# A decoder layer on one core: the causal convolution by three half-length filters, its tables and FF operands moved

## The chip, the core and the metric

The kernel runs on one core of one Trainium2 chip. Its time is device microseconds (us) of one launch, as the median of several runs; a profiled execution of the same program gives the trace. The engines are TensorE (PE; its weight loads are PEld), VectorE (DVE), ScalarE (ACT), GpSimd (POOL) and SyncE (SP), which here only issues DMAs. Each runs its own instructions in order and waits on semaphores that other engines raise.

## The reference

One layer over 1024 tokens with 1024 features, all in float32. Cut to what matters here:

```python
z = rms_norm(h, mix_norm_g) @ w_in                 # split into conv, mla, pool, gmlp columns
a, g = jnp.split(z_conv, 2, axis=-1)               # conv: 256 channels
y = a * jax.nn.sigmoid(g)
y = lax.conv_general_dilated(y, dw_w[:, None, :], window_strides=(1,), padding=[(30, 0)],
        feature_group_count=256, ...) + dw_b       # causal, 31 taps, each channel by itself
o_conv = jax.nn.silu(layer_norm(y, ln_g, ln_b)) @ pw_w
o_mla  = latent_attention(z_mla, cos(positions), sin(positions), ...)
o_pool, o_gmlp = multiscale_pool(z_pool, ...), spatial_gating(z_gmlp, ...)
h = h + concat(rms_norm of each group) @ w_out
h = h + square(relu(rms_norm(h) @ w_ff1)) @ w_ff2  # 1024 -> 4096 -> 1024
out = rms_norm(h, final_norm_g)
```

## The kernel before

Every matmul keeps float32 accuracy by three passes (`mm3`): each operand is split into a high part (a ScalarE copy) and a low part (a VectorE subtraction; `split`, lines 130 and 131, or `split_scaled`, 134 and 135), and high x high, high x low and low x high are summed in PSUM. So every weight slab and every activation that TensorE reads costs one ScalarE and one VectorE instruction first.

**Stage 1**, to about 395 us, is all that precedes the FF part. The input projections come group by group: convolution (tiles `zc`, gated by `conv_gate` into `ycv`), pooling (`zp`), gating (`zgm`, two 128-token tiles at a time by `z_mm`), latents (`zml`). Weights come through a ring of two raw buffers (`load_raw`) on SP's queue and are split into slots of a ring of ten (`wslot`). The convolution holds channels on partitions (two tiles of 128, index `i`) and tokens along the free axis, in two halves of 512 (`hf`). A tap is one fused multiply-add of up to 512 columns with a per-channel weight (`lag`, `conv_taps`, line 337). Of the 31 taps, lag 0 is a ScalarE instruction (`tap0`); of the second channel tile 7 taps of the first half and 13 of the second (`NPT`) are a ScalarE multiplication and a GpSimd addition each (`pool_taps`, lines 328 and 329); the other 100 are VectorE's. The taps of the first half need only the first half's gating. Then `conv_ln` (layer norm over channels: transposes to tokens, statistics, back), `conv_out` (the pointwise matrix `cw`), and `wo_tile(0, ...)`, the convolution group's share of the output projection. The pooling windows are sums by doubling on GpSimd (`addsh`, line 355). The rotary table `CS` is made of positions by ten elementwise instructions (lines 383 to 392), six of them on GpSimd, and is read by `latent_T` and `q_prep`.

In stage 1 the order on each engine is not written by hand: a planner takes the program's order as priority, `tc.high_priority(offset=n)` lifts a block by n, and it places whatever its own estimate of times says is ready. The calls stand in lines 1256 to 1466.

**The FF part** has an order written by hand (`run`, in steps of 12 matmuls 128x512 for the first product and 12 per output tile for the second). Each step issues, in this order: weight loads for eight steps ahead, the `post` of the step before (evictions), the operand splits of four steps ahead, its own `now` list, the `split` of the step before, its matmuls. The first product uses Strassen's seven products on 2x2 blocks: tokens in two halves, features in two halves. For the first 12 pairs of weight blocks, `early` runs the two products that need only the first tokens (steps 0 to 23). Meanwhile `hn_T1`, `hn_T1_split`, `combine` and `combine_split` make the other token operands. `f_relu` evicts and squares, `f_parts` splits the result into a tile `fst` and GpSimd's queue stores it (`fs`); `f_store` stores it unsplit (`fr`). `h_away` stores four tiles of h that are not needed for a while. The second product runs in chunks of four pairs (`Chunk`), whose operands are loaded on SP's queue: tokens `fs` (0, 1, 3), weights `w1` and `w2`, unsplit tokens `f1` and `f2`. The loads of the first chunk are spread over the last steps of the first product (`tail2`, `tail`).

## Time and profile before

| | us |
|---|---|
| median of 3 runs | 1042.67 (1041.95 to 1043.56) |
| the profiled execution | 1039.44 |
| its span, first to last instruction | 1037.7 |

The mean granted TensorE clock is 0.985 of full. Busy time of TensorE is modelled from pipelined matmuls, so that "busy" is not yet "at full rate"; a count of matmuls in a stretch says more. "Idle before" in a row of a group is the time that the engine stood idle just before these instructions, and the arrow names what ended it. In a row of waits, "A line <- B line" means that A stood until B was done.

### The profile page before, as it was taken

To read this page: it belongs to the slowest core of one execution; us is meant where nothing else is said; L and a number is where in the kernel's file an instruction comes from. 1 tells how busy PE (TensorE), PEld (TensorE's weight loads), DVE (VectorE), ACT (ScalarE), POOL (GpSimd) and SP (SyncE) were. 2 spreads that over 40 slices of the span, in tenths; PEclk is the share of its full clock that TensorE was granted. 3 is DMA by queue.
4 is the path that set the end of the run, shared out by engine and by line. 5 is a ranking of instruction groups with operands and counts; after the bars stand their busy time and mean duration, and the time that the engine had idled before them with its cause. 6 is when DMAs were issued, how large, how long until landed. Compare 5 with 4: busy or idle time off the path is not lost.

```text
span 1037.7 us, 13384 instructions
## 1 busy us (share of the span) xinstructions
PE 992.7 (96%) x4674; PEld 817.8 (79%) x4674; DVE 846.3 (82%) x1276; ACT 502.3 (48%) x937; POOL 246.8 (24%) x333
## 2 busy tenths in 40 slices
PE   9994899999999999988999999999999999999996
PEld 7883689888888887867888887887888888888885
DVE  5999999998888765987677775656998988988997
ACT  7641147556657765754545444453341431431424
POOL 0459558423232312222121111211000000000005
PEclk9997899999999999999999999999999999999998
DMA  9411015210002006866666675559858258258004
GB/s 334 165 56 37 32 54 185 82 41 23 19 1 82 1 1 216 298 246 219 235 217 230 233 235 185 220 181 414 337 189 298 82 181 306 81 180 326 1 1 163
DMA packets 49492, 165.71 MB, mean 160 GB/s; under 512 B 6032, under 2 KB 7952, under 8 KB 49424
## 3 DMA queue, kind: packets, MB, share of 16 engines
q1 hardware_dynamic: 36288, 119.68, 33.1%
q0 software_dynamic: 12992, 45.10, 11.1%
q8 instruction: 37, 0.61, 0.2%
q14 instruction: 31, 0.25, 0.1%
q10 hardware_dynamic: 144, 0.07, 0.0%
HBM read 113.45 MB, written 51.38 MB: 159 GB/s over the span
## 4 chain that ended last, share of the span: by engine, by line
PE 65%; DVE 16%; issue 6%; DMA 5%; ACT 4%; POOL 3%; SPq 0%; POOLq 0%; DVEq 0%; ACTq 0%
PE ffb L160 16%; PE ffx L160 13%; PE ffa L160 12%; DVE acc L337 8%; PE ffy L160 8%; PE wo L160 4%; PE ob L160 2%; PE s L676 2%; PE zc L160 2%; DMA raw_b<-in_w_ff 2%; DMA fs<-fst 1%; PE ptb L719 1%; PE woa L160 1%; PE qb L160 1%; DVE h L475 1%
## 5 line engine op out<-in xcount | busy, mean ns | idle before, releaser
L160 PE MATMUL ffb<-wop,fop 128*128 128x512 f32 x756 | 178.3, 395 | 0.0
L160 PEld LDWEIGHTS ffb<-wop,fop 128*128 128x128 f32 x756 | 142.1, 188 | 34.2
L160 PE MATMUL ffx<-hnT,wop 128*128 128x512 f32 x624 | 149.4, 392 | 0.8 <-DVE s L944 0.8
L160 PE MATMUL ffa<-wop,fop 128*128 128x512 f32 x576 | 137.3, 397 | 2.4 <-DVE h L1083 1.9
L160 PEld LDWEIGHTS ffx<-hnT,wop 128*128 128x128 f32 x624 | 117.0, 188 | 27.2 <-DVE s L944 1.2
L884 DVE TENSOR_TENSOR wop<-w_raw,wop 128x512 fp32r<-128x512 f32 x112 | 76.1, 688 | 68.3 <-ACT wop L881 68.3
L160 PEld LDWEIGHTS ffa<-wop,fop 128*128 128x128 f32 x576 | 109.2, 190 | 28.6 <-DVE h L1083 2.4
L881 ACT ACTIVATE wop<-raw_b 128x512 fp32r<-128x512 f32 x96 | 59.6, 623 | 122.9 <-PE ffa L160 44.3
L337 DVE SCALAR_TENSOR_TENSOR acc<-ycv,cols,acc 128x512 f32<-128x512 f32 (+22 forms) x100 | 99.1, 1032 | 0.7 <-ACT acc L317 0.4
L881 ACT ACTIVATE wop<-w_raw 128x512 fp32r<-128x512 f32 x112 | 68.8, 626 | 43.8 <-DVE w_raw L1027 18.9
L881 ACT ACTIVATE fop<-raw_f 128x512 fp32r<-128x512 f32 x64 | 39.8, 623 | 74.7 <-DVE h_back L1083 27.6
L160 PE MATMUL ffe<-hnT,wop 128*128 128x512 f32 x288 | 70.5, 402 | 4.4 <-ACT m L980 4.4
L1243 POOL TENSOR_SCALAR mr_ms<-mssq,epsr 128x1 f32<-128x1 f32 x7 | 2.8, 401 | 296.9 <-ACT fjunk L1241 296.9
L884 DVE TENSOR_TENSOR wop<-raw_b,wop 128x512 fp32r<-128x512 f32 x96 | 65.6, 684 | 9.3 <-ACT wop L881 8.6
L160 PEld LDWEIGHTS ffe<-hnT,wop 128*128 128x128 f32 x288 | 54.4, 191 | 17.0 <-ACT m L980 5.2
L160 PE MATMUL ffy<-hnB,wop 128*128 128x512 f32 x192 | 46.9, 393 | 2.8 <-ACT s L980 2.8
L160 PE MATMUL ffy<-hnT,wop 128*128 128x512 f32 x192 | 46.6, 391 | 0.0
L958 POOL DMA_DIRECT2D fs<-fst x48 | 25.8, 538 | 87.1 <-DVE fst L131 83.7
L160 PEld LDWEIGHTS ffy<-hnB,wop 128*128 128x128 f32 x192 | 36.0, 188 | 11.3 <-ACT s L980 3.2
L884 DVE TENSOR_TENSOR fop<-raw_f,fop 128x512 fp32r<-128x512 f32 x64 | 43.9, 686 | 0.0
L160 PEld LDWEIGHTS ffy<-hnT,wop 128*128 128x128 f32 x192 | 36.2, 189 | 8.1
L329 POOL TENSOR_TENSOR acc<-acc,tap 128x512 f32<-128x512 f32 (+7 forms) x20 | 35.0, 1749 | 28.9 <-ACT tap L328 27.6
(453 smaller groups left out, 2157.2 us busy)
## 6 DMA issues: line engine op xcount, KB each, us to landing
fs<-fst POOLq DMA_DIRECT2D x48, 512.0 KB, 3.4
fop<-fs SPq DMA_DIRECT2D x48, 512.0 KB, 7.2
w_raw<-in_w_ff SPq DMA_DIRECT2D x44, 512.0 KB, 4.4
raw_b<-in_w_ff SPq DMA_DIRECT2D x32, 512.0 KB, 5.9
raw_f<-fr SPq DMA_DIRECT2D x32, 512.0 KB, 5.7
fr<-s POOLq DMA_DIRECT2D x32, 256.0 KB, 3.2
fr<-f POOLq DMA_DIRECT2D x20, 256.0 KB, 2.4
xin<-in_x SPq DMA_DIRECT2D x8, 512.0 KB, 8.7
```

Of the source, the lines that this page charges most:

```text
L160: pe.matmul(out, lhs(x), rhs(y), start=start and i == 0, stop=stop and i == 2, skip_group_check=more)
L329: pool.tensor_tensor(aa, aa, tap, ALU.add)
L337: dve.scalar_tensor_tensor(aa, ya, c, aa, ALU.mult, ALU.add)
L475: dve.scalar_tensor_tensor(h[t], b, rs, h[t], ALU.mult, ALU.add)
L676: pe.matmul(sb_[:, c0:c0 + w], q[:, x, qo:qo + P], kt[:, y, 0:w], start=i == 0, stop=i == 2 and not last)
L719: pe.transpose(b[:, place[j] + s * P:place[j] + (s + 1) * P], pts[s][:, (2 * kp + j) * P:(2 * kp + j + 1) * P], ident)
L881: act.activation(self.t[:, 0], self.src(), AF.Copy)
L884: dve.tensor_sub(self.t[:, 1], self.src(), high(self.t))
L958: pool.dma_start(fs[p][q], t.rearrange("p x c -> p (x c)").bitcast(F32))
L1243: pool.tensor_scalar(ms, ssq, epsr[:, t:t + 1], 1.0, ALU.add, ALU.mult)
```

## The change

- **Convolution.** Even and odd tokens are kept as two planes of 512 (`conv_gate` writes them so, and builds the gate product in its PSUM bank). The even outputs are x0 * even taps + x1 (one step later) * odd taps; the odd outputs follow from (x0 + x1) * (even + odd taps) minus the two products. That makes three filters of 16, 15 and 16 taps over 512 columns per channel tile. All taps but two per tile run on VectorE; GpSimd has none. The block is placed, at normal priority, where the second half of the taps stood, and all four `conv_ln` after it; `cw` is loaded after them.
- **Position table.** Its six GpSimd instructions become six on VectorE.
- **Order of stage 1.** `gmlp(0)` stands after two more projections; two latent slabs (`zml` 2 and 3) use a raw buffer of another ring, and slab 3 has a higher priority.
- **FF.** `hn_T1` and its split run at steps 3 + 2j and 4 + 2j instead of 7 + 2j and 8 + 2j, `combine` and its split at 12 + 2j and 13 + 2j instead of 15 + 2j and 16 + 2j, `h_away` at step 4 instead of 5. The squaring of the early products goes from VectorE to ScalarE. `fst` of pairs 1 and 2 uses the ring of ten and not the single buffer `CS`. Of the first chunk's `fs` 1 loads, two go behind the `w2` loads.

```diff
-        dve.scalar_tensor_tensor(ycv[i][:, sl], ba, 0.5, rb[:, sl], ALU.mult, ALU.mult)
+        dve.scalar_tensor_tensor(ba, ba, 0.5, rb[:, sl], ALU.mult, ALU.mult)
         act.activation(th, th, AF.Tanh, scale=0.5)
-        dve.scalar_tensor_tensor(ycv[i][:, sl], th, 1.0, ycv[i][:, sl], ALU.add, ALU.mult)
+        dve.scalar_tensor_tensor(ycv[i].rearrange("p c n -> p n c")[:, hf * 256:(hf + 1) * 256],
+                                 th.rearrange("p (n c) -> p n c", c=2), 1.0,
+                                 ba.rearrange("p (n c) -> p n c", c=2), ALU.add, ALU.mult)
...
-    for hf in range(2):
-        tap0(0, hf)
-        tap0(1, hf)
-        pool_taps(hf, NPT[hf])
...
+    def conv_sums():
+        for i in range(2):
+            q = C_DWW + i * CK + 1
+            w = cols[:, q:q + CK - 1].rearrange("p (m c) -> p m c", c=2)
+            dve.tensor_add(hsum[:, i * (CK // 2):(i + 1) * (CK // 2)], w[:, :, 0], w[:, :, 1])
+
+    def chain(out, src, taps):
+        for k, c in taps:
+            dve.scalar_tensor_tensor(out[:, k:], src[:, 0:512 - k], c, out[:, k:], ALU.mult, ALU.add)
+
+    def conv_even_odd(i):
+        x0, x1 = ycv[i][:, 0], ycv[i][:, 1]
+        y0, y1 = acc[i][:, 0], acc[i][:, 1]
+        b = E("conv_b")
+        act.activation(y0, x0, AF.Copy, scale=tap(i, 0))
+        act.activation(b, x1, AF.Copy, scale=tap(i, 1))
+        chain(y0, x0, [(k, tap(i, 2 * k)) for k in range(1, CK // 2 + 1)])
+        chain(b, x1, [(k, tap(i, 2 * k + 1)) for k in range(1, CK // 2)])
+        bias = cols[:, C_DWB + i:C_DWB + i + 1]
+        dve.scalar_tensor_tensor(y1, y0, bias, b, ALU.subtract, ALU.add)
+        dve.tensor_scalar(y0[:, 0:1], y0[:, 0:1], bias, None, ALU.add)
+        dve.scalar_tensor_tensor(y0[:, 1:], y0[:, 1:], bias, b[:, 0:511], ALU.add, ALU.add)
+        dve.tensor_add(x0, x0, x1)
...
+        dve.scalar_tensor_tensor(y1, x0, both(0), y1, ALU.mult, ALU.subtract)
+        chain(y1, x0, [(k, both(k)) for k in range(1, CK // 2)] + [(CK // 2, tap(i, CK - 1))])
...
-    pool.tensor_scalar(ang, kq, cols[:, C_INVF:C_INVF + 1], 1.0, ALU.mult, ALU.mult)
-    pool.tensor_scalar(kq, ang, 1.0 / TWO_PI, cols[:, C_PHN:C_PHN + 1], ALU.mult, ALU.add)
-    pool.tensor_scalar(kq, kq, 1.0, MAGIC, ALU.mult, ALU.add)
-    pool.tensor_scalar(kq, kq, 1.0, -MAGIC, ALU.mult, ALU.add)
+    dve.tensor_scalar(ang, kq, cols[:, C_INVF:C_INVF + 1], None, ALU.mult)
+    dve.tensor_scalar(kq, ang, 1.0 / TWO_PI, cols[:, C_PHN:C_PHN + 1], ALU.mult, ALU.add)
+    dve.tensor_scalar(kq, kq, MAGIC, None, ALU.add)
+    dve.tensor_scalar(kq, kq, MAGIC, None, ALU.subtract)
...
-    pool.tensor_scalar(ang, ang, 1.0, cols[:, C_PHASE:C_PHASE + 1], ALU.mult, ALU.add)
-    pool.tensor_scalar(ang, ang, 3.1415925, -3.1415925, ALU.min, ALU.max)
+    dve.tensor_scalar(ang, ang, cols[:, C_PHASE:C_PHASE + 1], 3.1415925, ALU.add, ALU.min)
+    dve.tensor_scalar(ang, ang, -3.1415925, None, ALU.max)
...
+        if name == "zml" and s > 1:
+            raw = U("O", "zml_raw", [1024])
+            nc.sync.dma_start(raw[:, :2 * width], src[s])
+            wz[name, s] = split_w(raw, 2 * width, name + str(s))
...
         act.activation(f, b, AF.Relu)
-        if mul:
-            dve.tensor_mul(f, f, f)
-        else:
-            act.activation(f, f, AF.Square)
+        act.activation(f, f, AF.Square)
...
-                f_parts(p, 0, self.f, slot("fst") if p > 2 else
+                f_parts(p, 0, self.f, slot("fst") if p else
                         sb.tile([P, 2, 512], F32R, tag="CS", name="fst", bufs=1))
...
     with tc.high_priority(offset=2000):
-        conv_taps(0, NPT[0])
         z_load("zml", 2)
...
         load_wo(3, 0, dve)
+    with tc.high_priority(offset=4000):
         z_load("zml", 3)
     with tc.high_priority(offset=1000):
         load_wo(3, 1, pool)
-    with tc.high_priority(offset=300):
-        gmlp(0)
     z_mm("zgm", 1, 0)
     with tc.high_priority(offset=4000):
         z_mm("zml", 1, 1)
+    gmlp(0)
...
-    conv_ln(1)
-    with tc.high_priority(offset=4000):
-        conv_taps(1, NPT[1])
-        conv_ln(2)
+    conv_sums()
+    for i in range(2):
+        conv_even_odd(i)
+    for u in range(3):
+        conv_ln(u)
...
-        for f, s in ((hn_T1, 7 + 2 * j), (hn_T1_split, 8 + 2 * j), (combine, 15 + 2 * j), (combine_split, 16 + 2 * j)):
+        for f, s in ((hn_T1, 3 + 2 * j), (hn_T1_split, 4 + 2 * j), (combine, 12 + 2 * j), (combine_split, 13 + 2 * j)):
             steps[s].now.append(lambda j=j, f=f: f(j))
-    steps[5].now.append(h_away)
+    steps[4].now.append(h_away)
...
-    for t, n, name, ii in ((tail2, 1, "w1", (0, 1)), (tail2, 5, "w1", (2,)), (tail, 1, 1, range(4)),
-                           (tail, 2, "w1", (3,)), (tail, 2, 0, range(4)), (tail, 3, "w2", range(4)),
+    for t, n, name, ii in ((tail2, 1, "w1", (0, 1)), (tail2, 5, "w1", (2,)), (tail, 1, 1, (0, 1)),
+                           (tail, 2, "w1", (3,)), (tail, 2, 0, range(4)), (tail, 3, "w2", range(4)), (tail, 3, 1, (2, 3)),
```

## Rows read from the trace of the kernel before

**Rows 1.** The page: busy us of each engine (share of the span, instructions), and the granted TensorE clock in 40 slices of the span (tenths; 9 is 90% or more).

```profile
PE 992.7 (96%) x4674; PEld 817.8 (79%) x4674; DVE 846.3 (82%) x1276; ACT 502.3 (48%) x937; POOL 246.8 (24%) x333
...
PEclk9997899999999999999999999999999999999998
```

**Rows 2.** Busy time by stretch (us from the span's start): stretch and length, then busy us and instructions of PE, PEld, DVE, ACT and POOL, the granted clock, the DMA share and GB/s.

```profile
0.00:60.00 60.00, 57.76 (x255) 46.21 (x256) 46.72 (x63) 39.86 (x67) 14.12 (x16) 1.00 0.60 222
...
180.00:320.00 140.00, 138.73 (x771) 116.96 (x770) 121.91 (x202) 83.61 (x171) 45.77 (x62) 1.00 0.10 31
...
420.00:440.00 20.00, 20.00 (x97) 16.52 (x96) 19.90 (x33) 14.09 (x28) 5.36 (x10) 1.00 0.79 280
440.00:480.00 40.00, 33.60 (x138) 26.74 (x137) 33.00 (x53) 21.83 (x40) 8.59 (x16) 0.96 0.65 234
480.00:700.00 220.00, 219.22 (x955) 178.90 (x954) 146.56 (x226) 110.95 (x191) 43.09 (x80) 1.00 0.62 218
700.00:725.00 25.00, 22.64 (x92) 17.83 (x91) 15.28 (x25) 8.71 (x15) 3.77 (x7) 0.93 1.02 414
...
60.00:180.00 120.00, 99.17 (x480) 84.36 (x479) 118.84 (x148) 51.55 (x117) 86.46 (x78) 0.93 0.23 75
180.00:395.00 215.00, 211.35 (x1234) 180.57 (x1232) 174.38 (x284) 135.95 (x268) 65.41 (x98) 1.00 0.10 30
```

**Rows 3.** TensorE's waits from 60 to 180 us: us in total, times, longest.

```profile
PE zgm L160 <- DVE zgm2l L131: 9.5, 1, 9.5
PE lnb L541 <- DVE acc L337: 4.2, 1, 4.2
PE zgm L160 <- DVE zgm3l L131: 3.7, 1, 3.7
PE gate L490 <- DVE gv_l L131: 2.1, 2, 1.4
...
```

**Rows 4.** Busy time by short stretches at a lower granted clock (columns as in rows 2).

```profile
123.00:127.00 4.00, 4.00 (x12) 3.10 (x11) 4.00 (x6) 0.00 (x0) 0.00 (x0) 0.57 0.00 0
460.00:465.00 5.00, 4.65 (x13) 3.72 (x14) 4.65 (x8) 2.25 (x5) 1.07 (x2) 0.66 0.63 249
...
718.00:724.00 6.00, 4.07 (x12) 3.10 (x12) 5.14 (x9) 1.26 (x2) 0.54 (x1) 0.73 1.03 419
```

**Rows 5.** VectorE's groups by line (busy us, mean ns of one, idle before): from 0 to 395 us; then the taps from 0 to 60 us; last, by the view of stretches, VectorE's busy time on taps alone from 60 to 180 us (with their count, the clock, the DMA share and GB/s).

```profile
L337 DVE SCALAR_TENSOR_TENSOR acc<-ycv,cols,acc 128x512 f32<-128x512 f32 (+22 forms) x100 | 99.1, 1032 | 0.7 <-ACT acc L317 0.4
...
L131 DVE TENSOR_TENSOR zgm2l<-zgm_raw,zgm2h 128x1024 fp32r<-128x1024 f32 x1 | 2.9, 2905 | 0.0
...
L131 DVE TENSOR_TENSOR zgm1l<-zgm_raw,zgm1h 128x1024 fp32r<-128x1024 f32 x1 | 1.2, 1218 | 0.0
...
L383 DVE CAST kq<-posi 128x1024 f32<-128x1024 int32 x1 | 0.7, 684 | 0.0
...
L337 DVE SCALAR_TENSOR_TENSOR acc<-ycv,cols,acc 128x504 f32<-128x504 f32 (+15 forms) x19 | 18.2, 965 | 0.7 <-ACT acc L317 0.4
...
60.00:180.00 120.00, 79.83 (x82) 0.93 0.23 75
```

**Rows 6.** GpSimd's groups by line to 395 us.

```profile
L329 POOL TENSOR_TENSOR acc<-acc,tap 128x512 f32<-128x512 f32 (+7 forms) x20 | 35.0, 1749 | 28.9 <-ACT tap L328 27.6
...
L384 POOL TENSOR_SCALAR ang<-kq,cols 128x1024 f32<-128x1024 f32 x1 | 1.6, 1568 | 0.9 <-DVE kq L383 0.9
```

**Rows 7.** Timeline of VectorE and of GpSimd: start us, us, instruction, count.

```profile
34.71 3.10 DVE L337 SCALAR_TENSOR_TENSOR acc<-ycv,cols,acc 128x511 f32<-128x511 f32 x4 [0.35 <-ACT acc L317]
...
61.95 0.68 DVE L250 SCALAR_TENSOR_TENSOR ycv<-th,ycv 128x512 f32<-128x512 f32 x1
62.56 4.64 DVE L337 SCALAR_TENSOR_TENSOR acc<-ycv,cols,acc 128x495 f32<-128x495 f32 x7
...
72.86 13.46 DVE L337 SCALAR_TENSOR_TENSOR acc<-ycv,cols,acc 128x492 f32<-128x492 f32 x8
...
102.14 2.35 DVE L337 SCALAR_TENSOR_TENSOR acc<-ycv,cols,acc 128x487 f32<-128x487 f32 x1
...
101.22 2.75 POOL L355 TENSOR_TENSOR win_b<-win_c 128x1022 f32<-128x1022 f32 x1
```

**Rows 8.** The instructions that read the rotary table and the layer-normed convolution (tiles `CS` and `pwc`): count, ns min/median/max, first and last start.

```profile
L591 DVE TENSOR_TENSOR tl<-ctb,CS x2: 695/696/696, 204.8 to 228.4; 64x512 f32<-64x512 f32 x2
...
L160 PE MATMUL pwc<-us_h,cw x16: 389/394/478, 233.9 to 249.8; 128*128 128x512 f32 x16
```

**Rows 9.** From 395 to 480 us: ScalarE's waits, TensorE's waits, and VectorE's squaring.

```profile
ACT hnT L825 <- DVE hnT L827: 8.5, 4, 2.7
ACT fst L130 <- DMA fs<-fst: 6.7, 2, 5.1
...
PE ffe L160 <- ACT m L980: 4.4, 2, 3.6
PE ffy L160 <- ACT s L980: 2.8, 1, 2.8
...
L951 DVE TENSOR_TENSOR fe<-fe 128x512 f32<-128x512 f32 x12 | 8.3, 688 | 6.7 <-ACT fe L949 6.7
```

**Rows 10.** At the start of the second product: TensorE's waits from 700 to 730 us, and ScalarE's timeline.

```profile
PE ffa L160 <- DVE h L1083: 1.9, 1, 1.9
...
716.76 0.63 ACT L881 ACTIVATE wop<-raw_b 128x512 fp32r<-128x512 f32 x1 [3.49 <-DMA raw_b<-in_w_ff]
```

More of the change, by code (lines that the diff above doesn't have):

```diff
@@ L20 @@
 NM = 2
-NPT = (7, 13)
 NWARM = 16
@@ L111, in N, with E @@
         return sb.tile([P, 512], F32, tag="N", name=name, bufs=1)
+    def E(name):
+        return sb.tile([P, 512], F32, tag="e", name=name, bufs=1)
     def small(n, name, bufs=2):
@@ L300, in _trunk @@
     for i in range(2):
-        ycv[i] = U("P", "ycv%d" % i, [T])
+        ycv[i] = U("P", "ycv%d" % i, [2, 512])
+        acc[i] = U("K", "acc%d" % i, [2, 512])
     conv_gate(0, 0, b[:, 0:512], b[:, 512:])
@@ L324, in pool_taps @@
-    def pool_taps(hf, n):
-        for k in range(1, n + 1):
-            c, ya, aa = lag(1, k, hf)
-            tap = U("Z", "tap", [512])[:, :ya.shape[1]]
-            act.activation(tap, ya, AF.Copy, scale=c)
-            pool.tensor_tensor(aa, aa, tap, ALU.add)
-    def conv_taps(hf, n):
-        todo = [(0, k) for k in range(1, CK)]
-        for j, k in enumerate(range(n + 1, CK)):
-            todo.insert(2 * j + n + 1, (1, k))
-        for i, k in todo:
-            c, ya, aa = lag(i, k, hf)
-            dve.scalar_tensor_tensor(aa, ya, c, aa, ALU.mult, ALU.add)
@@ L339, in _trunk, with tap @@
-    for hf in range(2):
-        tap0(0, hf)
-        tap0(1, hf)
-        pool_taps(hf, NPT[hf])
+    def tap(i, lag_):
+        q = C_DWW + i * CK + CK - 1 - lag_
+        return cols[:, q:q + 1]
+    hsum = const([P, 2 * (CK // 2)], "hsum")
+    def conv_sums():
[3 more added lines that the diff above has]
+            dve.tensor_add(hsum[:, i * (CK // 2):(i + 1) * (CK // 2)], w[:, :, 0], w[:, :, 1])
@@ new lines, in chain, with both @@
+    def chain(out, src, taps):
[14 more added lines that the diff above has]
+        dve.tensor_add(x0, x0, x1)
+        def both(k):
+            m = (i + 1) * (CK // 2) - 1 - k
+            return hsum[:, m:m + 1]
+        dve.scalar_tensor_tensor(y1, x0, both(0), y1, ALU.mult, ALU.subtract)
+        chain(y1, x0, [(k, both(k)) for k in range(1, CK // 2)] + [(CK // 2, tap(i, CK - 1))])
@@ L398, in z_load @@
         src, width = {"zgm": (a["w_gm"], 512), "zml": (a["w_ml"], 352)}[name]
-        wz[name, s] = load_w(src[s], 2 * width, name + str(s))
+        if name == "zml" and s > 1:
+            raw = U("O", "zml_raw", [1024])
+            nc.sync.dma_start(raw[:, :2 * width], src[s])
+            wz[name, s] = split_w(raw, 2 * width, name + str(s))
+        else:
+            wz[name, s] = load_w(src[s], 2 * width, name + str(s))
     def z_mm(name, hf, jp):
@@ L541, in conv_ln @@
                 pe.transpose(b[:, j * GW + ct * P:j * GW + (ct + 1) * P],
-                             acc[ct][:, (2 * u + j) * P:(2 * u + j + 1) * P], ident)
-        st = small(12, "bst", 2)
+                             acc[ct][:, j, u * P:(u + 1) * P], ident)
+        st = small(12, "bst", 1)
         mv = small(4, "bmv", 2)
@@ L851, in spare @@
         return sb.tile([P, 2, 512], F32, tag="CS", name=name, bufs=1)[:, 0]
-    def E(name):
-        return sb.tile([P, 512], F32, tag="e", name=name, bufs=1)
     def dram(name, n, dt=F32):
@@ L1294, in _trunk @@
         z_mm("zml", 1, 1)
+    gmlp(0)
     with tc.high_priority(offset=300):
         load_wo(2, 0, dve)
-    with tc.high_priority(offset=1000):
-        cw = small_w(load_raw(a["conv_pw"], 512, "cw_raw"), 512, "K", "cw")
     with tc.high_priority(offset=300):
         wq = load_w(a["w_uq"], 1024, "wq", None, pool)
-    with tc.high_priority(offset=1000):
-        conv_ln(0)
     with tc.high_priority(offset=2000):
@@ L1323, in _trunk @@
     conv_ln(3)
+    with tc.high_priority(offset=1000):
+        cw = small_w(load_raw(a["conv_pw"], 512, "cw_raw"), 512, "K", "cw")
     kr_prep(0, K)
```

22 lines of the change are left out of this document (7 added, 15 removed).

## The prediction

> **What bounds the kernel now.** I read the page's busy lines first, then stretches of the span, then TensorE's waits, then the lines of the engine those waits name. TensorE (PE) is busy nearly everywhere, and its granted clock is below full in few slices [rows 1]. A stretch with nothing wrong is 480 to 700 us: 955 matmuls in 220 us, clock 1.00 [rows 2]. So only TensorE's gaps can be won, and they lie in three places. Stage 1 (projections to attention, up to about 395 us): VectorE (DVE) is busy 118.8 of 120 us between 60 and 180 us, and there TensorE has only 99.2 us [rows 2]. The waits of that stretch name VectorE: 9.5 us for the low half of a gating weight, 4.2 for the convolution's sums, 3.7 and 2.1 for other low halves, 19.5 us in all [rows 3]. After waits the clock falls to the lower level (1.2 of 2.4 GHz) for some microseconds. In 123 to 127 us it averages 0.57, which costs (1 - share) x length = 1.7 us [rows 4]. Over 60 to 180 us the mean is 0.93, 8.4 us of lost clock [rows 2]; what falls on the waits costs nothing more, and I count 4.8 (three such dips). So stage 1 can give back at most 19.5 + 4.8 = 24.3 us before 180 us. The second place is 440 to 480 us, the third 700 to 725 us; both below.
>
> **Convolution.** Removed are 100 VectorE taps, 99.1 us [rows 5], and 20 adds on GpSimd (POOL), 35.0 us [rows 6], with their ScalarE multiplications. Added per channel tile are 15 taps for the even filter, 14 for the odd one, 1 + 15 for the summed one and 3 full-length combinations: 48, so 96 ops of about 512 columns, and four tiny ones. The count hardly falls; the price of one does. Taps that alternate between two accumulators took 4.64 us for 7, or 0.66 each; four that each read the one before took 3.10, or 0.78; eight beside GpSimd's adds took 13.46, or 1.68 [rows 7]. A tap beside a 2.75 us window add took 2.35 [rows 7]. The new chains are dependent ones, but the planner may put other work or the other chain between: 96 x 0.66 = 63.4 to 96 x 0.78 = 74.9 us; I take 70, nearer the dependent rows. The eight window adds of the pooling branch stay, and each can stretch one op by 1.7 us: 0 to 13.5, taken as 10, since a busy VectorE is nearly always in an op. Ops that stood beside the removed adds shrink, such as the low half of zgm2 from 2.9 to the 1.2 us of zgm1's [rows 5]; with three or four smaller ones I take 5 (0 to 7).
>
> The Trainium skill (SBUF — State Buffer, "Who interferes with whom") says that a VectorE instruction with two SBUF inputs contends with a GpSimd instruction that reads SBUF, and that one of them waits for the whole of the other. By that rule the new taps stay exposed to the window adds, as the 2.35 us tap shows [rows 7]; it speaks against counting all 96 at the clean price. The same section lets one-input VectorE ops lock GpSimd out as well, so the moved tables could delay the windows; the sum by it would be a few microseconds on an engine with idle time.
>
> **Position tables.** Six one-input ops of 128x1024 move to VectorE. GpSimd's first took 1.6 us [rows 6]. VectorE has no such op here: the one-input cast of the same shape took 0.68, a two-input op (zgm1's low half) 1.22 [rows 5]; 4.1 to 7.3 us, taken as 4.5 because the cast is the nearer kind. Their results are read by a multiplication that first runs at 204.8 us [rows 8], so they hide.
>
> **Sum for VectorE.** -99.1 + 70 + 10 - 5 + 4.5 = -19.6 us; at best -99.1 + 63.4 + 0 - 7 + 4.1 = -38.6, at worst -99.1 + 74.9 + 13.5 + 7.3 = -3.4. Busy time up to 395 us is 46.7 + 118.8 + 174.4 = 339.9 [rows 2], so it becomes 320.
>
> **What that is worth in stage 1.** The new convolution can't start before both gatings of both halves are done, 62.6 us [rows 7]; the 18.2 us of taps before 60 us [rows 5] move behind that. Before 60 us VectorE then does 28.5 us, and if it stays full to 180 us another 118.8, leaving 320 - 147 = 173, about what is left at 180 us now (174.4). But TensorE is then up to 24.3 us further on, because its weights are no longer queued behind stretched taps. In 180 to 320 us VectorE worked 121.9 of 140 us (87%) while TensorE was busy 138.7 [rows 2]: that share is sustainable. 173 / 0.87 = 199, so stage 1 ends at 379 and not 395: **16 us**. Bounds: 24.3 us if TensorE alone binds; 1 us if VectorE keeps its 81% of 180 to 395 us (173 / 0.81 = 214).
>
> **Moves inside stage 1.** The gating group now stands behind two projections. Its gate waited 2.1 us [rows 3]; those projections need only weights, so TensorE has work meanwhile: counted in the 16. Two slabs of the latent weights load into a buffer of another ring, one of them at a raised priority, ahead of others on SP's queue; DMA is mostly idle there (share 0.23 in 60 to 180 us [rows 2]), so at nothing. The convolution's layer norm and its weight `cw` come later. The first matmul that reads them is at 233.9 us [rows 8], which with VectorE done by about 190 leaves some 20 us. If that cover is gone each microsecond is paid. PSUM: the gate product is now built in its bank, which holds it for about one Tanh and one VectorE op more; X has two banks, so at nothing. Strided writes in four gate ops and in the layer norm: 0 to 1 us, taken as 0.
>
> **First FF four stretches.** `hn_T1` and its splits move four steps up, `combine` three, `h_away` one; the square of the early products goes from VectorE (12 x 0.69 = 8.3 us [rows 9]) to ScalarE, for about as much there; only the first split result is still built in the single buffer. Now ScalarE stands 6.7 us for the DMA out of that buffer, 5.1 in one piece [rows 9]. Then VectorE is full (19.9 of 20 us in 420 to 440 [rows 2]), ScalarE waits for it 8.5 us, and TensorE pays: 3.6 us for a copy of `m`, then 2.8 for a copy that itself waited for the store of the last early product [rows 9], plus 0.34 x 5 = 1.7 us of low clock in 460 to 465 [rows 4]. Together 8.1 us. Both engines get room: VectorE was busy 52.9 of 60 us in 420 to 480 and loses some 8; ScalarE was busy 35.9 and can take them [rows 2]. The stores on GpSimd's queue follow sooner; the four `hs` stores go onto SP's queue one step sooner, in front of weights that are fetched eight steps ahead. I take **7 us**, range 2 to 8; the rest is left for the first steps, which now carry the VectorE work of `hn_T1`.
>
> **Start of the second FF product.** Two of four token loads go behind the four w2 loads on SP's queue. There the DMA is the limit (share 1.02 in 700 to 725 us [rows 2]). ScalarE waits 3.5 us for the first w2 slab until 716.8, and TensorE then 1.9, with 0.27 x 6 = 1.6 us of low clock [rows 4, 10]. Moving 1 MB behind, at 414 GB/s [rows 2], lets that slab land 2.5 us sooner. 0 to 3.5 us, **3** taken. The two late tokens are wanted only by the third product.
>
> **Sum.** 16 + 7 + 3 = 26. The profiled execution (span 1037.7, 1039.4 with what lies around it) becomes about 1013.4; it lay 3.2 below the median 1042.7, so the median becomes **1016.7**, given as 1017.
>
> **Rivals.** (a) VectorE binds: the new chains cost their dependent price and keep meeting the window adds, so stage 1 gives 1 to 4 and the rest 7 to 10: 1029 to 1035. For it: remaining work at 180 us is as large as now. Against: the 35.0 us of GpSimd adds that stretched taps are gone [rows 6]. The rule on the shared inputs above bears on this one. (b) All of TensorE's stalls go, 24.3 + 8 + 3.5 = 36: 1007, down to 1000 if the later waits thin out too. (c) **Slower:** the planner starts the chain late, for it now stands behind the gating groups and a weight split, without the raised priority it had. Without taps VectorE has about 118.8 - 79.8 = 39 us of work in 60 to 180 [rows 2, 5], a third; two thirds idle is lost. It then ends at 379 + 0.62 us for each microsecond of lateness (a full microsecond, less the third done meanwhile at 87%). From 26 us late (start after 88 us) stage 1 loses; with the 10 elsewhere it is slower from about 42 us late (start after 105). At 120 us it ends at 415: 1042.7 + 20 - 10 = 1053. Against it: operands are ready at 62.6 and the planner fills idle engines. (d) It does what it says but moves waits elsewhere: the later attention waits take the place of the early ones, and 10 are lost there too: 1041 to 1044.
>
> **How the numbers follow.** Forecast, 1008 to 1027: 0.56; (a) 0.17; (b) 0.12; (c) 0.11; (d) 0.04. Faster by over 0.2%, about what a measurement of this kernel can tell from no change (2.1 us): 0.85; within: 0.04; slower: 0.11. The range for 8 in 10 takes the forecast, (a) and most of (b): 1002 to 1035.
>
> **What would show it.** Right: taps near 0.7 us with a few of 2 us; the wait for zgm2's low half gone; first FF steps starting near 379 us; the clock at full up to 180 us; no 3.6 us gap near 440; w2's slab landing before TensorE's third M1 tile. Wrong: VectorE full past 200 us with TensorE waiting on evictions (a), VectorE idle after 63 us (c), new waits of TensorE in the first FF steps or behind layer norm.

## Result and profile after

| | before | after |
|---|---|---|
| median time, us | 1042.31 (1041.26 to 1043.56, 4 runs) | 1030.03 (1028.41 to 1031.63, 4 runs) |
| span of the profiled execution, us | 1037.7 | 1029.8 |
| ratio | | 0.9882, 95% interval 0.9858 to 0.9906 |
| VectorE busy in 0 to 395 us | 339.9 | 319.6 |
| last projection of the attention output ends (tile `woa`), us | 391.45 | 391.30 |
| first product out of the FF starts (tile `ffy`), us | 464.80 | 459.18 |
| second product starts (tile `ffa`), us | 711.82 | 704.45 |
| last matmul of the kernel ends, us | 1028.95 | 1021.46 |

Faster by 12.3 us, where 25.7 were forecast. The profiled executions differ by 7.8 only (1039.4 and 1031.6 with what lies around their spans): that of before lay under its median, that of after over it. What these two traces show of the gain arises between 391 and 712 us. Stage 1, which should have given 16, ends where it ended. One trace tells its end to some 2 us only: `changed_again`, `conv_only` and `steps_undone` below run the instructions of after in the same order in stage 1, and their `woa` ends at 389.8, 390.4 and 389.2 us; `ff_only`, with the stage 1 of before, ends it at 392.9. By the mean of each kind stage 1 ends 2.0 us sooner than before.

The page's busy lines after ([rows 1] are those of before), and the granted clock in 40 slices. VectorE has 27.6 us less, TensorE as much as before (992.7). The slices of lower clock moved from the fourth and fifth (78 to 130 us) to the eighth and ninth (180 to 232 us).

```profile
PE 993.3 (96%) x4674; PEld 817.0 (79%) x4674; DVE 818.7 (79%) x1270; ACT 497.2 (48%) x929; POOL 203.1 (20%) x307
PEclk9999999889999999999999999999999999999999
```

Stretches after, in the columns of [rows 2]; the last two rows are new.

```profile
0.00:60.00 60.00, 57.43 (x247) 45.93 (x248) 37.40 (x58) 35.44 (x60) 2.74 (x9) 0.97 0.67 243
60.00:180.00 120.00, 111.91 (x565) 95.92 (x564) 113.37 (x161) 48.71 (x121) 63.54 (x70) 1.00 0.23 79
180.00:320.00 140.00, 129.34 (x693) 107.65 (x692) 116.40 (x200) 78.10 (x154) 36.28 (x50) 0.94 0.06 19
320.00:395.00 75.00, 72.72 (x466) 63.68 (x465) 52.45 (x83) 52.42 (x98) 19.83 (x36) 1.00 0.09 28
160.00:200.00 40.00, 31.71 (x141) 24.64 (x141) 35.96 (x51) 12.25 (x27) 12.04 (x14) 0.95 0.12 40
200.00:212.00 12.00, 7.83 (x24) 6.06 (x24) 9.90 (x21) 9.11 (x15) 1.78 (x4) 0.50 0.00 1
```

In 60 to 180 us TensorE did 111.9 us of work (99.2 before) at full clock: the waits of [rows 3] on the gating weights are gone. In 180 to 320 us it did 129.3 where it had done 138.7, and the clock was 0.94. From 200 to 212 us it was at its lower level, 0.50. So the stall was moved, not removed: the matmul that has 700 recorded ahead of it starts at 153.1 us (174.7 before, 21.6 sooner), the one with 800 at 178.4 (193.7), with 900 at 211.6 (213.4), with 1400 at 304.6 (304.5).

TensorE's longest waits from 150 to 240 us after (us in total, times, longest):

```profile
PE lnT L577 <- DVE yn L572: 3.8, 1, 3.8
PE lnT L577 <- ACT us_h L132: 3.7, 1, 3.7
PE wo L162 <- DVE h L495: 1.9, 2, 1.0
```

The last tap ends at 192.7 us, and the layer norms of the convolution come right behind it, one after the other. VectorE's tap groups after, from 0 to 200 us (busy us, mean ns of one, idle before); [rows 5] has the 99.1 us of before:

```profile
L336 DVE SCALAR_TENSOR_TENSOR acc<-ycv,cols,acc 128x497 f32<-128x497 f32 (+14 forms) x32 | 29.3, 951 | 0.0
L336 DVE SCALAR_TENSOR_TENSOR conv_b<-ycv,cols,conv_b 128x511 f32<-128x511 f32 (+13 forms) x28 | 22.7, 810 | 0.2
L336 DVE SCALAR_TENSOR_TENSOR acc<-ycv,hsum,acc 128x511 f32<-128x511 f32 (+13 forms) x28 | 22.6, 807 | 0.2
```

The groups overlap at their edges: line 336 as a whole is busy 73.3 us. With the eight other full-length operations (lines 347 to 356), 5.9 us, the convolution takes about 79 us; the forecast was 70 + 10. VectorE's idle time lies elsewhere now. ScalarE's timeline, then VectorE's, of after from 65 to 85 us (start, us, instruction, idle before and its releaser):

```profile
75.08 1.07 ACT L132 ACTIVATE zgm3h<-zgm_raw 128x1024 fp32r<-128x1024 f32 x1 [8.70 <-PE zp L162]
76.05 1.32 ACT L342 ACTIVATE acc<-ycv,cols 128x512 f32<-128x512 f32 x2
```
```profile
68.89 0.72 DVE L336 SCALAR_TENSOR_TENSOR conv_b<-ycv,cols,conv_b 128x498 f32<-128x498 f32 x1
73.88 0.18 DVE L375 TENSOR_TENSOR rc<-win_b,cols 128x16 f32<-128x16 f32 x1 [4.28 <-POOL win_b L371]
...
77.85 3.04 DVE L336 SCALAR_TENSOR_TENSOR acc<-ycv,cols,acc 128x511 f32<-128x511 f32 x2
```

The copies that begin the even filters stand on ScalarE's queue behind the high half of zgm3, which waits 8.7 us until the pooling projection's matmuls (`zp`) are done. When the first odd filter ends at 69.6 us, VectorE has no tap to do and waits for a window sum; the even filters begin at 77.85. Before, the first tap began at 34.7 [rows 7].

To see what that is worth I cut VectorE's time at one point, the start of the matmul with 900 recorded ahead of it (it lies among the layer norms of the convolution or shortly behind them); from it to the end of `woa` the kernels of the table below need 178 to 183 us. VectorE's busy time up to it, before and after:

```profile
0.00:80.00 80.00, 77.07 (x337) 61.48 (x337) 66.72 (x82) 50.91 (x82) 29.39 (x24) 1.00 0.49 180
80.00:213.38 133.38, 112.70 (x563) 96.61 (x564) 130.07 (x180) 58.43 (x137) 85.07 (x91) 0.94 0.23 76
```
```profile
0.00:80.00 80.00, 77.43 (x334) 62.34 (x335) 52.45 (x73) 39.72 (x65) 13.87 (x17) 0.98 0.55 199
80.00:211.57 131.57, 114.96 (x568) 97.59 (x567) 124.22 (x190) 55.66 (x132) 56.52 (x70) 0.94 0.19 65
```

Before: 196.8 us busy and 16.6 idle make 213.4. After: 176.7 busy and 34.9 idle make 211.6. The work fell by 20.1 us, as forecast (19.6); idle time grew by 18.3, of it 14.3 before 80 us.

Behind the point it is the other way round. From there to the end of `woa` TensorE (first busy time of a row) is busy all but 2 to 4 us, and VectorE (third) has 142 us of work, in before, in after and in a kernel that leaves most taps out (`no_taps`, run 7):

```profile
213.38:391.45 178.07, 175.71 (x1054) 151.10 (x1053) 141.86 (x232) 115.25 (x227) 50.46 (x74) 1.00 0.08 25
```
```profile
211.57:391.30 179.73, 176.06 (x1054) 151.17 (x1053) 141.67 (x237) 116.39 (x229) 50.77 (x76) 1.00 0.08 24
```
```profile
187.48:365.68 178.20, 175.69 (x1054) 151.00 (x1053) 142.02 (x234) 114.79 (x226) 51.73 (x76) 1.00 0.08 25
```

In the FF the waits of [rows 9] have shrunk (TensorE's waits in 395 to 480 us; 4.4 and 2.8 us before), and in the second product a new one stands (the third row, from the view of 690 to 740 us):

```profile
PE ffe L162 <- ACT m L996: 0.8, 1, 0.8
PE ffy L162 <- ACT s L996: 0.4, 1, 0.4
```
```profile
PE ffb L162 <- DMA fop<-fs: 2.2, 3, 1.5
```

### The profile page after: what moved, and what is told of

Its sections match the earlier page's. It is cut to its first block, busy times and chain, and to the rows that moved or that the text cites. A ratio compares the mean times of both kernels' runs of the same rounds, so it can differ in the third digit from the quotient of the medians.

```text
span 1029.8 us, 13319 instructions
## 1 busy us (share of the span) xinstructions
PE 993.3 (96%) x4674; PEld 817.0 (79%) x4674; DVE 818.7 (79%) x1270; ACT 497.2 (48%) x929; POOL 203.1 (20%) x307
## 4 chain that ended last, share of the span: by engine, by line
PE 74%; DVE 11%; issue 4%; DMA 3%; POOL 3%; ACT 3%; SPq 0%; POOLq 0%; DVEq 0%; ACTq 0%
PE ffb L162 15%; PE ffx L162 13%; PE ffa L162 11%; PE ffy L162 8%; PE wo L162 5%; PE zc L162 4%; PE ffe L162 4%; DVE acc L336 3%; PE ob L162 3%; PE s L698 2%; DMA raw_b<-in_w_ff 1%; PE ptb L741 1%; DMA raw_f<-fr 1%; PE woa L162 1%; PE zp L162 1%
## 5 line engine op out<-in xcount | busy, mean ns | idle before, releaser
L162 PE MATMUL ffa<-wop,fop 128*128 128x512 f32 x576 | 135.2, 393 | 0.0
L900 ACT ACTIVATE fop<-raw_f 128x512 fp32r<-128x512 f32 x64 | 39.9, 623 | 74.3 <-DVE h_back L1099 27.5
L1140 DVE TENSOR_TENSOR raw_f<-raw_f,raw_f 128x512 f32<-128x512 f32 x48 | 32.7, 683 | 5.7 <-DMA raw_f<-fr 5.7
L721 POOL TENSOR_SCALAR P<-P,rr 128x384 f32<-128x384 f32 (+7 forms) x32 | 24.0, 752 | 57.6 <-DVE rr L720 57.5
```

The source lines that it names most:

```text
L162: pe.matmul(out, lhs(x), rhs(y), start=start and i == 0, stop=stop and i == 2, skip_group_check=more)
L721: pool.tensor_scalar(pt, pt, rr, 1.0, ALU.mult, ALU.mult)
L900: act.activation(self.t[:, 0], self.src(), AF.Copy)
L1140: dve.tensor_sub(self.r[d, i], self.r[x, i], self.r[y, i])
```

## Experiments

The theories that the expectations name:

- **G**: the layer norms, and the attention's preparation behind them, stand behind the late end of the convolution, and that place gives the lead back.
- **V**: VectorE is the bound up to the norms, and its work there counts, in whatever order.
- **S**, which came after the first four runs: as V, and VectorE's idle time before 80 us counts as much as work, because the filters start later than the taps did.
- **O**: TensorE's order in stage 1 decides, and a move only trades waits.
- **C**: what is taken off VectorE by giving it to GpSimd comes back as longer VectorE instructions.

Each ratio is to the kernel before, with its 95% interval.

**1. The FF part alone** (`ff_only`): the kernel before with `hn_T1`, `combine` and `h_away` sooner, the square on ScalarE, the slot for the split product, and the two late token loads.

```diff
-        if mul:
-            dve.tensor_mul(f, f, f)
-        else:
-            act.activation(f, f, AF.Square)
+        act.activation(f, f, AF.Square)
...
-        for f, s in ((hn_T1, 7 + 2 * j), (hn_T1_split, 8 + 2 * j), (combine, 15 + 2 * j), (combine_split, 16 + 2 * j)):
+        for f, s in ((hn_T1, 3 + 2 * j), (hn_T1_split, 4 + 2 * j), (combine, 12 + 2 * j), (combine_split, 13 + 2 * j)):
```

> The kernel before with the FF parts alone (square on ScalarE, the token part in its slot from the second group on, steps four sooner, the late token loads split): the convolution, its tables and the order of the gating groups are those of before. In the trace of after the first product out of the FF ends 5.6 us sooner and the fold 7.5 us sooner, and stage 1 ends at the same time as before, so both theories expect 5.6 to 7.5 us less than before: 1035 to 1037. If instead the convolution part gives something that only shows later, this run gives less than half of the change's 12.3 us, 1037 or more.

Measured: 1033.5 us, 0.9923 (0.9909 to 0.9936), 7.9 us less. The FF part brings what was expected and a little more, all by itself.

**2. The convolution part alone** (`conv_only`): the changed kernel with the FF edits of run 1 undone, line for line.

> The changed kernel with the FF parts undone: only the convolution, the position tables on VectorE and the gating groups' order are new. Stage 1 of after ends where it ended before (last attention matmul 391.45 against 391.30 us), so both theories expect 1040 to 1043. If the convolution brings something that stage 1's end doesn't show: 1037 or less.

Measured: 1039.4 us, 0.9976 (0.9962 to 0.9989), 2.1 us less. So the convolution part gives 1 to 4 us. The two ratios multiply to 0.990, which lies in the change's own interval.

**3. Layer norms ahead of the convolution's end** (`ln_reads_gate`).

```diff
-                             acc[ct][:, j, u * P:(u + 1) * P], ident)
+                             ycv[ct][:, j, u * P:(u + 1) * P], ident)
```

> The changed kernel whose layer norm transposes read the gated sequence in place of the convolution's result, so the convolution's output is left out of the result; all its taps still run on VectorE. Theory G (the lead is given back because the layer norms, and the attention preparation behind them, stand behind the late end of the convolution's serial chain): the norms come before the last chain, stage 1 ends 8 to 15 us sooner, 1015 to 1022. Theory V (VectorE's work up to the attention binds, in whatever order): the taps are all still there, 1028 to 1031.

Measured: 1036.9 us, 0.9958 (0.9942 to 0.9974), slower than the change. The norms did come sooner (their transposes at 174 to 202 us, 197 to 226 in after), and `woa` ended at 395.85, 4.6 us later. What VectorE did for the norms it didn't do for TensorE's evictions: from 150 to 240 us TensorE waited 8.0 us for `h` (1.9 in after). G falls in this form; V expected no change and doesn't explain the loss either.

**4. Both channel tiles' chains interleaved** (`side_by_side`): for each lag one tap of each filter of each tile, then the summed filters in the same way.

```diff
-    for i in range(2):
-        conv_even_odd(i)
+    conv_both()
```

> The changed kernel with the chains of both channel tiles interleaved, so that no tap reads what the tap just before it wrote and the layer norms follow an earlier end of the convolution; the number of taps and their sizes are the same. Theory G: the convolution ends 10 to 20 us sooner than 192.7 us and the time falls by 5 to 12 us against the changed kernel, to 1018 to 1025. Theory V: the same work on the same engine, 1028 to 1032.

Measured: 1037.0 us, 0.9956 (0.9942 to 0.9970). Both theories missed. All four first copies now stand behind zgm3's high half on ScalarE's queue, so the first tap began at 77.7 us (50.1 in after), and the last one ended no sooner (193.0 us); it is no test of G. VectorE was idle 36.8 us before 80 us instead of 27.5, and the norms' point came at 217.5 instead of 211.6. That pointed to S.

**5. The even filters' copies sooner** (`even_sooner`): `conv_even_odd`'s first line moves behind the gates.

```diff
         conv_gate(i, hf, ba, bg)
+        if hf:
+            act.activation(acc[i][:, 0], ycv[i][:, 0], AF.Copy, scale=tap(i, 0))
...
-        act.activation(y0, x0, AF.Copy, scale=tap(i, 0))
```

> The changed kernel with one thing moved: ScalarE's two copies that begin the even filters are issued right behind the gates, ahead of zgm3's high part, behind which they waited on ScalarE's queue until 76.05 us. Theory S (what VectorE was spared came out as idle time before 80 us: 14.6 us more of it than before in 20 to 80, because the filters need both halves of the sequence and the even ones start at 77.85): VectorE loses its idle time in 69.6 to 73.9 and the end of the convolution comes 5 to 10 us sooner, 1020 to 1026. Theory G (the layer norms' place behind the convolution is what counts): they move by the same 5 to 10 us and the time with them, 1020 to 1026. Theory O (the planner's order on TensorE decides; any move in stage 1 only trades one wait for another): 1028 to 1037.

Measured: 1025.2 us, 0.9846 (0.9825 to 0.9866). VectorE's idle time before 80 us fell from 27.5 to 22.4, the norms' point from 211.6 to 204.2, the end of `woa` from 391.3 to 385.9, the time by 4.8 (3.8 against `changed_again`). As S has it; O falls as a general rule.

**6. The first tile's filters by column halves** (`halves_sooner`), on `even_sooner`; each first copy comes by halves too, behind its gate.

```diff
+        for lo, hi in ((0, 256), (256, 512)) if i == 0 else ((0, 512),):
+            part(b, x1, [...], lo, hi)
+            part(y0, x0, [...], lo, hi)
```

> As the one before, and the first channel tile's even and odd filters are split into two column halves, so that the first halves start when the first half of the sequence is gated (near 36 us) and not at 50; 29 taps more in number, some 3 us of VectorE time more. Theory S: VectorE's idle time in 35 to 47 is used too, and the time falls further, 1015 to 1022. Theory O: 1028 to 1037.

Measured: 1026.2 us, 0.9849 (0.9830 to 0.9868). VectorE up to the norms' point:

```profile
0.00:80.00 80.00, 78.27 (x338) 63.09 (x339) 65.98 (x113) 40.41 (x68) 15.36 (x16) 1.00 0.54 195
80.00:199.99 119.99, 110.27 (x564) 94.57 (x563) 113.22 (x176) 53.85 (x132) 57.75 (x71) 0.99 0.22 74
```

Idle before 80 us is 14.0, as in the kernel before (13.3). Work is 179.2, and the point comes at 200.0, 4.2 sooner than with `even_sooner`; `woa` ends at 382.9, 2.9 sooner. But `even_tail`, which has `even_sooner`'s order in stage 1, has its point at 202.3 and `woa` at 383.6, and the timed executions don't differ (1023.4 to 1027.8 against 1023.3 to 1028.6): for the time inconclusive.

**7. One tap for each filter** (`no_taps`), in `chain`:

```diff
-        for k, c in taps:
+        for k, c in taps[:1]:
```

> The changed kernel in which each of the six filters keeps one tap; the other taps, some 70 us of VectorE's work, are left out of the result. Every theory that puts the end of stage 1 on VectorE expects TensorE to bind from there on: 1000 to 1015. If the taps are not what stage 1 waits for: 1025 to 1031.

Measured: 1006.7 us, 0.9661 (0.9647 to 0.9676). Busy time from 0 to 395 us:

```profile
0.00:395.00 395.00, 388.72 (x2093) 330.62 (x2094) 282.50 (x451) 235.51 (x467) 121.70 (x177) 1.00 0.27 93
```

TensorE is busy 388.7 of 395 us at full clock, and `woa` ends at 365.7, 25.6 us sooner than in after; up to there TensorE has 5.5 us of gaps. That is about the floor of stage 1 with this work on TensorE, and the forecast's upper bound of 24.3 us was its right size. Leaving out VectorE's taps alone gets there.

**8. Position tables back on GpSimd** (`tables_back`); the first of six lines:

```diff
-    dve.tensor_scalar(ang, kq, cols[:, C_INVF:C_INVF + 1], None, ALU.mult)
+    pool.tensor_scalar(ang, kq, cols[:, C_INVF:C_INVF + 1], 1.0, ALU.mult, ALU.mult)
```

> The changed kernel with the six position operations back on GpSimd: some 4.5 us less on VectorE between 96 and 120 us, and GpSimd busier there. Theory S, with VectorE busy without a break from 80 to 193 us: 2 to 5 us sooner, 1025 to 1028. Theory O: within 2 us of the changed kernel, or slower, 1028 to 1037.

Measured: 1031.8 us, 0.9904 (0.9890 to 0.9918); no gain. VectorE's work up to the norms' point fell by 2.5 us to 174.2, and idle time grew by 3.0: the latent products were held up, 6.5 us at 119 us until ScalarE had read the gating products out of their bank and 2.8 at 135 us for the low half of zml3. O's number: waits took the place of the work.

**9. Ten odd taps on ScalarE and GpSimd** (`pool_taps`), on `even_sooner`.

```diff
+    for k in range(1, 11):
+        z = U("Z", "tap", [512])[:, :512 - k]
+        act.activation(z, ycv[1][:, 1, 0:512 - k], AF.Copy, scale=tap(1, 2 * k + 1))
+        pool.tensor_tensor(acc[1][:, 1, k:], acc[1][:, 1, k:], z, ALU.add)
```

> The kernel even_sooner (1025.2) with ten of the second tile's odd taps made by ScalarE (multiplication) and GpSimd (addition), as the kernel before made twenty: 8 us less for VectorE, some 17.5 us more for GpSimd. Theory V (from 60 us to the end of the convolution VectorE is always busy, and each microsecond of its work there moves stage 1): 1017 to 1021. Theory C (VectorE's ops beside GpSimd's adds stretch by as much as is taken off): 1023 to 1030.

Measured: 1027.5 us, 0.9867 (0.9843 to 0.9892). VectorE's groups from 60 to 130 us by shape:

```profile
L338 DVE SCALAR_TENSOR_TENSOR acc<-ycv,cols,acc 128x501 f32<-128x501 f32 x3 | 5.5, 1817 | 0.0
...
L133 DVE TENSOR_TENSOR zgm3l<-zgm_raw,zgm3h 128x1024 fp32r<-128x1024 f32 x1 | 2.9, 2912 | 0.0
...
L387 DVE TENSOR_TENSOR rc<-win_b,cols 128x16 f32<-128x16 f32 x1 | 2.4, 2378 | 0.0
...
L338 DVE SCALAR_TENSOR_TENSOR conv_b<-ycv,cols,conv_b 128x500 f32<-128x500 f32 x1 | 2.4, 2361 | 0.0
```

Ten taps fewer, and VectorE's work up to the norms' point is 176.5 us (175.8 in `even_sooner`): several taps that take 0.73 us elsewhere take 1.8 to 2.4, zgm3's low half 2.9 instead of 1.2. C holds. The last three rows stood beside window additions of GpSimd, not beside the moved ones; those had only pushed the window additions some 8 us back (the last one starts at 104.1 us, 96.1 in `even_sooner`). The Trainium skill (SBUF — State Buffer, "Who interferes with whom") says that a VectorE instruction with two SBUF inputs contends with a GpSimd instruction that reads SBUF, and calls the port pair that they share an exclusive lock; these rows agree. The last tap ended 13.6 us sooner (166.2 against 179.8 us) and `woa` no sooner (387.9; 385.9 and 383.6 with the stage 1 of `even_sooner`), so the convolution's end alone doesn't set it.

**10. Twelve taps more** (`taps_more`), on `even_sooner`.

```diff
+        if i == 0:
+            chain(b, x1, [(k, tap(i, 2 * k + 1)) for k in range(1, 13)])
```

> The kernel even_sooner (1025.2) with twelve taps more in the first tile's odd filter (lags that it has already, so the output is another): 9 to 10 us more work for VectorE. Theory V: 1032 to 1036. If stage 1's end has slack against VectorE, as it must have if the order or the layer norms set it: 1024 to 1028.

Measured: 1037.1 us, 0.9959 (0.9946 to 0.9972), 11.9 more than `even_sooner`. VectorE's work rose by 9.9 us, the norms' point by 11.4, the end of `woa` by 10.4. There is no slack against VectorE.

**11. Late tokens ahead of w2** (`even_tail`), on `even_sooner`.

```diff
-(tail, 3, "w2", range(4)), (tail, 3, 1, (2, 3)),
+(tail, 3, 1, (2, 3)), (tail, 3, "w2", range(4)),
```

> The kernel even_sooner (1025.2) with the two late token loads ahead of the four w2 loads instead of behind them. In the changed kernel TensorE waits 3.2 us at the second product for tokens that come by DMA. If those waits are what the moved loads cost: 2 to 3 us sooner, 1022 to 1024, with a wait for w2 of up to 1.9 us as before's in its place; if the DMA's share there only passes the wait on: 1024 to 1026.

Measured: 1025.7 us, 0.9849 (0.9831 to 0.9866). TensorE's waits from 690 to 740 us, first of `even_sooner`, then of this one:

```profile
PE ffb L162 <- DMA fop<-fs: 2.7, 2, 2.4
```
```profile
PE ffa L162 <- DVE h L1100: 5.2, 1, 5.2
```

The wait for tokens goes and one of 5.2 us for `h` comes; the first `w2` slab lands at 703.9 us, 698.6 in `even_sooner`. The load order there only passes a wait on. In its trace the second product even takes 2.5 us longer (320.4 against 317.9 us); stage 1 of that one execution was as much shorter.

**12. Token operands back in their steps** (`steps_undone`).

```diff
-        for f, s in ((hn_T1, 3 + 2 * j), (hn_T1_split, 4 + 2 * j), (combine, 12 + 2 * j), ...
+        for f, s in ((hn_T1, 7 + 2 * j), (hn_T1_split, 8 + 2 * j), (combine, 15 + 2 * j), ...
-    steps[4].now.append(h_away)
+    steps[5].now.append(h_away)
```

> The changed kernel (1030.0) with the token halves' splits and the combination back in the steps where they were; the square on ScalarE and the slot for the split product stay. If the earlier steps bring most of the FF part's 5.6 us: 1034 to 1036. If the square and the slot bring it: 1030 to 1032.

Measured: 1038.6 us, 0.9975 (0.9962 to 0.9989), 8.5 more than the change. TensorE's waits from 395 to 480 us:

```profile
PE ffy L162 <- ACT s L996: 4.7, 1, 4.7
PE ffe L162 <- ACT m L996: 1.5, 1, 1.5
```

Both waits of before are back, in other sizes. The square and the slot alone bring nothing; the earlier steps bring the FF's gain, with those two in place.

**13. The changed kernel again** (`changed_again`), as the base of the last three runs.

> The changed kernel as it is, as a base on the same chip: 1028 to 1032.

Measured: 1029.1 us, 0.9881 (0.9865 to 0.9897).

**14. A late start** (`start_late`): the odd filters' first coefficient takes zero times a value of zgm3's low half.

```diff
+        dve.tensor_scalar(tap(i, 1), wz["zgm", 3][:, 1, 0:1].bitcast(F32), 0.0, tap(i, 1), ALU.mult, ALU.add)
         act.activation(b, x1, AF.Copy, scale=tap(i, 1))
```

> The changed kernel in which the odd filters' first copy needs a value from zgm3's low part (times zero, so the result is the same): no tap can start before 77 us. The 16 taps that VectorE does before then, 11.7 us, come later, and VectorE stands idle in their place. Theory S (idle time of VectorE before 80 us costs stage 1 about its own length): 9 to 13 us more than the changed kernel, 1039 to 1043. If VectorE's early idle time is not what counts: 1028 to 1032.

Measured: 1041.5 us, 0.9999 (0.9988 to 1.0010), 12.4 more than the base on the same chip: one late operand costs as much as the whole change gained. VectorE up to the norms' point:

```profile
0.00:80.00 80.00, 77.68 (x342) 62.57 (x343) 45.05 (x61) 39.04 (x64) 14.97 (x18) 1.00 0.56 200
80.00:222.90 142.90, 116.41 (x561) 98.55 (x560) 131.22 (x203) 55.54 (x132) 61.35 (x69) 0.90 0.17 59
```

Work 176.3 as in after; idle 35.0 before 80 us and 11.7 behind it, 11.8 more than in after, and the point comes 11.3 later. S as expected.

**15. Norms ahead, once the idle time is used** (`norms_even`): the edit of run 3 on `even_sooner`.

> The kernel even_sooner (1025.2) whose layer norm transposes read the gated sequence instead of the convolution's result, so the convolution's output is left out of the result; all taps still run. Theory G for what is left of the loss (the norms stand behind the convolution): 5 to 10 us sooner, 1015 to 1020. Theory V (VectorE's work up to the norms is the same, whatever order): 1023 to 1028; later still if the norms push evictions back, as in ln_reads_gate.

Measured: 1030.9 us, 0.9894 (0.9876 to 0.9912), 5.7 more than `even_sooner`. The transposes ran at 171 to 196 us instead of 192 to 215, and `woa` ended at 388.1 us (385.9 and 383.6 with the stage 1 of `even_sooner`). G falls in this form too: norms that come 20 us sooner bring nothing. What takes the 5.7 us is not shown.

**16. Halves and tables together** (`halves_tables`).

> The kernel halves_sooner (1026.2) with the six position operations back on GpSimd. Theory V: VectorE, full from 35 us on, has 4.5 us less to do, 1021 to 1024. Theory C (ops beside GpSimd's stretch by what is saved, as in pool_taps): 1024 to 1029.

Measured: 1024.6 us, 0.9846 (0.9829 to 0.9862); on the same chip the change has 0.9881 (0.9865 to 0.9897). `woa` ends at 379.6. VectorE's work up to the norms' point was 180.4 us, so the tables took nothing off it, as C has it; idle before 80 us was 13.1. It has the lowest median of the kernels here that leave nothing out, 16.7 us under before and 4.4 under the change, but is not told apart from `even_sooner`, which only moves two copies.

The account of VectorE at the norms' point, worked out from each trace's windows as above (us):

```
kernel          point   busy  idle<80  idle later  woa ends
no_taps         187.5  118.8   35.8      32.9       365.7
halves_sooner   200.0  179.2   14.0       6.8       382.9
halves_tables   200.3  180.4   13.1       6.9       379.6
even_sooner     204.2  175.8   22.4       6.0       385.9
pool_taps       205.7  176.5   21.7       7.5       387.9
norms_even      206.1  176.8   19.8       9.5       388.1
after           211.6  176.7   27.5       7.3       391.3
tables_back     212.0  174.2   27.9       9.9       391.4
ln_reads_gate   212.4  174.0   26.5      11.9       395.9
before          213.4  196.8   13.3       3.3       391.5
taps_more       215.5  185.7   21.5       8.3       396.3
side_by_side    217.5  171.8   36.8       8.9       397.9
start_late      222.9  176.2   35.0      11.7       401.7
```

Busy and idle make up the point by arithmetic. What makes it an account is that three of the edits changed mainly one entry and the point followed, the time too: idle time down (`even_sooner`), work up (`taps_more`), idle time up (`start_late`). Each row is one execution. Traces of kernels with the same stage 1 differ by up to 1.9 us in the point and 2.3 in `woa`, so rows that lie closer are not told apart.

## Why the prediction failed, step by step

**VectorE's sum: right.** 320 us up to 395 were forecast, 319.6 came; the convolution's operations with their stretching cost about 79 where 80 were taken. The six position operations took 0.68 to 0.74 us each, 4.3 in all, where 4.5 were taken.

**What that is worth in stage 1: wrong, and this is the step that failed.** Up to 180 us the forecast held: VectorE had done 150.8 us (147 forecast), 169 were left (173), and TensorE was far ahead. From there I went on by "that share is sustainable. 173 / 0.87 = 199, so stage 1 ends at 379": VectorE would keep the share of 180 to 320 us because TensorE was up to 24.3 us further on. It kept 168.9 of 215 us, 0.79, below even the 0.81 of the lower bound. TensorE's lead did not last: its next work, the norms and the attention's preparation, needs what VectorE had left to do, and at 180 us VectorE had nearly as much left as before. I wrote that myself ("about what is left at 180 us now") and didn't draw the conclusion. What the runs put in its place is the account above: the norms' point moves with VectorE's work plus its idle time, and behind it come 178 to 183 us of which TensorE is busy 175 to 178 in every kernel. There VectorE's share, 142 us of 180, is no limit of its own, so dividing its work by a share could not give the end of the stage. The 20 us of work were spared, and 18 us of idle time came for them. The forecast had counted idle time, 31.5 us of it before 60 us (22.6 came, 13.3 before), but took it to be made up behind 180 us. The convolution part was worth 2.1 us where 16 stood.

**The start.** The forecast had the filters begin once both halves are gated, at 62.6 us. The odd ones began at 50.1, the even ones at 77.9, behind a weight on ScalarE's queue that the text didn't look at. That a later start is dear was in rival (c), at 0.62 us for each microsecond behind 62.6; `start_late` paid 12.4 us for 11.8 us of idle time, about one for one.

**Rivals.** Rival (a)'s time came, 1029 to 1035, with its split (stage 1 gives 1 to 4, the rest 7 to 10) and its head, VectorE binds; its reason, dear taps, did not, since they cost what was forecast. For TensorE, (d) tells what is seen in stage 1 (the early waits return later), but the FF's gain that it gave away stayed.

**FF stretches: right.** 7 were forecast, the FF part alone gave 7.9, by the earlier steps (`steps_undone`); from the end of `woa` to the start of `ffa` the traces have 320.4 us before and 313.2 after. That the square relieves the engines was not shown: it brings nothing without the earlier steps, and the steps without it were not run.

**Start of the second product: wrong in the sum.** Forecast 3, came 0: from the start of `ffa` to the end the kernel takes 317.1 us before and 317.0 after. At its place the gain did come: the first product of the chunk (`ffa`, up to the start of `ffb`) takes 10.9 us where it took 15.4. The next loads take it back, for the DMA is full here (share 1.03 from 704 to 715 us). By the kernel the two late tokens are read by the second of the chunk's seven products, not the third as the text said; they land at 714.2 and 716.5 us, and that product runs its 48 matmuls without a wait. TensorE then stands for the tokens of the third (`fs` 3), which are issued behind the other loads and land from 728.06 us on. TensorE's timeline, then SP's:

```profile
715.33 11.36 PE L162 MATMUL ffb<-wop,fop 128*128 128x512 f32 x48
728.20 0.94 PE L162 MATMUL ffb<-wop,fop 128*128 128x512 f32 x3 [1.51 <-DMA fop<-fs]
```
```profile
717.86 4.18 SPq L1121 DMA_DIRECT2D fop<-fs  x4
```

With the order turned round (`even_tail`) the wait stands at the first product instead, and the time is the same.

**Cover.** The late norms were to hide ahead of the first reader of their result, at 233.9 us [rows 8]. That reader even starts at 229.0 us, but TensorE stood 3.8 and 3.7 us for the norms' own transposes, with the clock at its lower level; those the text didn't price.

Left open: why the rest of stage 1 behind the norms' point varies by some 5 us between kernels (178 to 183), more than the traces of one stage 1 differ, and how much of the later idle time (6 to 12 us) is the norms' chain. What `even_sooner` and `halves_sooner` differ by is not settled either. A VectorE load between none (`no_taps`) and that of `even_sooner` was reached by no kernel here, since what GpSimd took over came back in VectorE's own instructions.

## What to carry to other kernels

Where one engine is full up to some point of the program, add up its work **and** its idle time to that point; work that is taken off it counts only if the rest can start as early as before. A form that needs more of its input before it can begin paid for that about one for one here, so look first at what starts the chain and at what stands ahead of that first operation in the other engine's queue. A lead of another engine in the middle of a stage is not yet a gain: ask what its next work needs, and when the full engine delivers it. And look for the point behind which another engine is the full one; a share of the first engine's busy time across that point says nothing of either part.

## What the runs showed of the hardware

Moving ten additions to GpSimd took ten taps, some 8 us, off VectorE and left its busy time up to the norms' point as it was (176.5 us, 175.8 in `even_sooner`); `rc<-win_b`, 16 columns, took 0.18 us in after and 2.38 beside a window addition of 2.78. The same shows with nearly all taps gone: in `no_taps` the two combinations of line 349, 511 columns, took 2.25 and 2.61 us beside window additions of 2.24 and 2.70 us, and 0.73 each in after. Executions of one kernel spread by up to three quarters of a per cent: those of `pool_taps` lie between 1023.5 and 1031.1 us. Gains of 1 to 3 us are therefore not told by four or five executions, nor by one trace, whose stage 1 ends within some 2 us.
